# Who makes the lo parts of the q, k and v blocks, and how much dense product goes between the steps of the 16x16 inverses

## The chip, the cores and the metric

The kernel runs on one core of a Trainium2 chip. The metric is device time in microseconds (us) of one execution, lower is better. The engines are TensorE (PE: matrix products; PEld is its loading of weights), VectorE (DVE), ScalarE (ACT), GpSimd (POOL) and SyncE (SP, which here only issues transfers). Each engine has its own list of instructions.

## The reference

One layer of a mixed block on 512 tokens of width 1024: a token mixer, a cross-attention to a memory of 256 rows, and a mixture of 32 experts, each followed by a layer norm. The token mixer starts with one wide projection and has two branches. The branch that matters here is a gated delta rule in chunks. In short:

```python
proj = h @ w_in                                   # 512 x 8744
qkv  = silu(causal_dwconv(concat(g_q, g_k, g_v), conv_w))
q, k = l2_normalize(q) * dk**-0.5, l2_normalize(k)
a_mat = where(strict, (k @ k.T) * decay, 0) * beta
sol   = triangular_solve(a_mat + I, [v * beta, k * beta * exp(gc)])
# then a scan over chunks: v_new = u - w @ state;  o = q_dec @ state + qk @ v_new;  state = ...
```

For each of 8 heads and each chunk a unit lower triangular matrix has to be inverted, or solved with. The other branch is sparse attention (compressed, selected and windowed keys). Its projections come out of the same wide product.

## The kernel before, in words

**Dense products.** `w_in` is cut into blocks of 256 or 260 columns. Float32 precision is had with three passes: the weights and the activations are each written as a hi part and a lo part, and `mm3` (L209 to L213) multiplies hi by hi, hi by lo and lo by hi. One block is loaded by `load_w` (L140): a transfer of 1 MB into a raw buffer (L144, on SP's queue), then `split` for the parts: ScalarE writes the hi part (L138), and an engine named in the call subtracts it from the raw data to get the lo part (L139). The buffers come from a pool of 21 (`B8`, `NB8`), which hold also the matrices of the delta rule.

**The list of blocks.** `dense` (L187) is a generator that goes through the list `blocks`. It asks for the load of block j+1 when it starts block j, then yields after each step of block j. A step is one `mm3`: for a block worked by channel (the q, k, v blocks, C_K, C_V, S_K, W_K) it is 128 by 128 by 512 and counted as 0.65 us, with two column groups (c = 0 and 1) of 8 steps each; for a block worked by token (S_V, W_V) it is 256 columns wide and counted as 0.32 us, with 32 steps. The order of the first blocks is z3, k00, k01, S_V, W_V, q00, q01, v00, v01, k10, k11, q10, C_V, q11, v10, v11, C_K, S_K, W_K. In a name such as q01 the first digit is the half of the heads, the second the block in that half. After the 8 steps of one column group of a q, k or v block `conv_silu` (L417) follows: one ScalarE instruction (L421), three of VectorE (L424), one of ScalarE (L427), one of VectorE (L428), and then a set of four transposes on TensorE (L217). The product of a column group lies in one of two PSUM buffers ("mm").

**The weave.** `Weave.chain` runs another generator (the delta rule's inverse, its scan, later the sparse attention) and, at each of its yields, takes steps from `dense` until their counted time uses up the yielded number. `W.until(label)` works dense steps off until the named block is through. The part of the program that the change touches is

```python
W.until("k01");  W.chain(gdn_inverse(0), "k11")
W.until("v01");  W.chain(gdn_scan(0), "q11")
W.until("k11");  W.chain(gdn_inverse(1), "n6160")
W.until("v11");  W.chain(gdn_scan(1))
```

**The inverse.** `gdn_inverse` (L473) works on four heads at once. It first makes the decay and the matrices AN, with a yield of ZA after each of four heads. Then it inverts all the 16x16 diagonal blocks by forward substitution, 15 steps of one VectorE multiplication (L534) and one VectorE sum (L535), each waiting for the one before; after every third step it yields ZB, five times in all. Two passes then spread the result into the block layout (L542 to L547: XC and then XTC), with a yield of ZC after each. Then TensorE's part begins: 128 small products of 32x32 (L554), which need XC, and in further stages (L560, L564, L575, L584, L589, L596, L605) the 32x32 blocks become the full 128x128 inverse, with yields ZD, ZE and fixed ones. GpSimd masks the blocks for L554 (L520) and clears XT (L521).

```python
for c in range(1, 16):
    V.tensor_tensor(tv, yb[:, 0:c, 0:c], nb[:, c, 0:c, None]..., op=OP.mult)   # L534
    V.tensor_reduce(yb[:, c, 0:c], tv..., axis=AX.X, op=OP.add)                 # L535
    if c % 3 == 0:
        yield ZB
```

**What sets the order.** The program is written down in the order of the weave; a planner then fixes each engine's list at build time, by the order in the text and by when it expects each instruction's data to be ready. On the chip every engine works its list off.

**POOL_PARTS.** Ten blocks (q00, q01, v00, v01, k10, k11, q10, q11, v10, v11) have their lo part made by GpSimd, all others by VectorE; the choice is made in `dense` at the call of `load_w`.

Of the kernel before, what the change touches and what calls it, by code (L numbers as in the profile page):

```python
# [91 lines left out]
def _body(ctx, tc, nc, I, O, dbg):  # L92
# [28 lines left out]
    def B8(shape, dt=FT):  # L121
        return big.tile(shape, dt, name="b8", bufs=NB8)
# [18 lines left out]
    def load_w(src, c0, n, eng=V, loads=1, splits=1):  # L141
        raw = B8([128, KD, WB])
        for k in pieces(loads):
            nc.sync.dma_start(raw[:, k, :n], src[128 * k.start:128 * k.stop, c0:c0 + n].rearrange("(k p) c -> p k c", p=128))  # L144
        hi = B8([128, KD, WB], FR)
        lo = B8([128, KD, WB], FR)
        for k in pieces(splits):
            split(hi[:, k, :n], lo[:, k, :n], raw[:, k, :n], eng)
        return hi, lo
# [23 lines left out]
    def dense(blocks, cur=None):  # L173


        load = lambda b: load_w(*b[1:4], eng=G if b[0] in POOL_PARTS else V, splits=SPL.get(b[0], 1))
        cur = cur or load(blocks[0])
# [686 lines left out]
    def nsa():  # L864
        wait, n = [], 0
        for h in range(H):
            W.until(HEAD[h])
            if h == 6:
                MT.update((n_, [B8([128, 4, S], FR) for _ in range(2)]) for n_ in "hl")
                MT["w"] = load_w(I["w_out"][0], 0, 256, eng=G if "w" in POOL_PARTS else V)  # L870
            for t in range(NT):
# [760 lines left out]


SPL = {"k00": 2}
ZA, ZB, ZC, ZD, ZE = 2.0, 2.5, 1.5, 1.4, 2.0
NB8, KBACK, PSP = 21, 6, 12
KB_LAST, KD_LAST = 3, 7
L0, L1 = 6, 8
# [3 lines left out]

GATES = ("m0", "z0", "m4", "m1", "m5", "z1", "m2", "z2", "m6", "m3", "m7")
HEAD = ("m4", "m5", "z1", "m2", "m6", "m3", "m7", "m7")
POOL_PARTS = ("q00", "q01", "v00", "v01", "k10", "k11", "q10", "q11", "v10", "v11")

_INS = ["x", "mem", "positions", "w_in", "gdn_conv_w", "gdn_a_log", "gdn_dt_bias", "gdn_norm_w", "cmp_pe", "cmp_w1",
        "cmp_b1", "cmp_w2", "w_out", "ln1_g", "ln1_b", "xa_wq", "xa_wkv", "xa_wo", "ln2_g", "ln2_b", "moe_w_group",
# [14 lines left out]
```

## Time and profile before

| | us |
|---|---|
| median of 3 runs | 1255.44 (1253.97 to 1255.5) |
| the profiled execution, its own time | 1254.66 |
| its span, first to last instruction | 1252.9 |
| TensorE busy in it | 1161.7 |
| VectorE busy | 658.2 |
| ScalarE busy | 459.3 |
| GpSimd busy | 181.9 |

The profile shows one execution. Its busy times are sums over the whole span; a stretch of the span has limits of its own, which the views by stretch (busy time of each engine, and the TensorE clock that was granted, as a share of full speed) and the lists of waits show. A wait "A <- B" is time in which A's engine had nothing running and B's instruction ended it. The delta rule's first inverse lies at about 59 to 138 us of the span, its first scan at 164 to 209, the second inverse at 210 to 304, the second scan from there to about 350.

### The profile page before, as it was taken

The page shows a single profiled execution, that of the slowest core. Times are in us where ns is not written, and L with a number is a line of the kernel's source. Part 1 is how long each engine was busy: PE and PEld are TensorE (multiplying, and loading weights), DVE is VectorE, ACT ScalarE, POOL GpSimd, SP SyncE. Part 2 cuts the span into 40 slices and gives each one's busy share as a digit, 9 for nine tenths or more (in the row PEclk, how much of TensorE's full clock was granted, in tenths as well). Part 3 has the DMA queues.
Part 4 walks back from the last instruction along what each step waited for, and adds up shares of the span by engine and source line. Part 5 has one row for each costly group of instructions (what it writes and reads, how often), then busy time and mean ns, then how long its engine had stood idle before and what let it go on. Part 6 is the DMA issues. An engine that isn't in the chain of part 4 may idle for free. (4 is left out here: it accounts for less than half of the span.)

```text
span 1252.9 us, 20776 instructions
## 1 busy us (share of the span) xinstructions
PE 1161.7 (93%) x8356; PEld 925.4 (74%) x8356; DVE 658.2 (53%) x1657; ACT 459.3 (37%) x1093; POOL 181.9 (15%) x151
## 2 busy tenths in 40 slices
PE   6996998879999999999899899999989999999994
PEld 6885787758888879999798799789985455455532
DVE  4695477874775724556457758233484111111147
ACT  4643454534544214343345524334142111111224
POOL 4151221221000000000001102000020000000185
PEclk9998999989999999999899999999998999999997
DMA  8220212112142562212531343227546899999823
GB/s 268 68 68 3 68 34 69 34 35 69 39 131 69 173 212 69 69 35 67 187 93 58 122 120 101 68 67 255 204 145 248 302 384 380 407 392 379 338 77 133
DMA packets 101882, 189.22 MB, mean 151 GB/s; under 512 B 10246, under 2 KB 74438, under 8 KB 97680
## 3 DMA queue, kind: packets, MB, share of 16 engines
q1 hardware_dynamic: 93456, 181.58, 41.1%
q0 software_dynamic: 2224, 3.94, 1.0%
q10 hardware_dynamic: 6096, 2.27, 0.8%
q8 instruction: 68, 1.11, 0.4%
q14 instruction: 38, 0.31, 0.1%
HBM read 177.93 MB, written 13.63 MB: 153 GB/s over the span
## 5 line engine op out<-in xcount | busy, mean ns | idle before, releaser
L211 PE MATMUL mm<-b,b 128*128 128x256 f32 (+3 forms) x1216 | 404.2, 333 | 21.7 <-ACT b L138 7.2
L212 PE MATMUL mm<-b,b 128*128 128x256 f32 (+3 forms) x1216 | 392.2, 323 | 2.2 <-DVE b L139 2.2
L213 PE MATMUL mm<-b,b 128*128 128x256 f32 (+3 forms) x1216 | 391.5, 322 | 0.7 <-POOL b L139 0.4
L211 PEld LDWEIGHTS mm<-b,b 128*128 128x128 f32 x1216 | 233.1, 192 | 43.3 <-issue 17.1
L213 PEld LDWEIGHTS mm<-b,b 128*128 128x128 f32 x1216 | 233.1, 192 | 22.1 <-issue 3.8
L212 PEld LDWEIGHTS mm<-b,b 128*128 128x128 f32 x1216 | 233.7, 192 | 18.2 <-DVE b L139 2.8
L1447 PE MATMUL ga<-b,b 128*64 128x512 f32 x512 | 131.5, 608 | 6.8 <-DVE b L1334 6.8
L139 DVE TENSOR_TENSOR b<-b,b 128x2048 fp32r<-128x2048 f32 (+4 forms) x48 | 101.8, 2123 | 56.5 <-ACT b L138 48.0
L138 ACT ACTIVATE b<-b 128x2048 fp32r<-128x2048 f32 (+4 forms) x58 | 104.3, 1799 | 26.9 <-DMA b<-in_w_in_dram 7.4
L1447 PEld LDWEIGHTS ga<-b,b 128*64 128x64 f32 x512 | 38.4, 138 | 73.8 <-issue 64.1
L424 DVE SCALAR_TENSOR_TENSOR t<-mm,cw,t 128x511 f32<-128x511 f32 (+2 forms) x72 | 53.8, 747 | 32.3 <-ACT t L421 31.1
L217 PE MATMUL tp<-cs,b 128*128 128x128 f32 x376 | 59.4, 287 | 9.7 <-DMA cs<-in_cst_dram 5.9
L1462 PE MATMUL ga<-b,t 128*64 128x512 f32 x256 | 63.9, 593 | 0.5 <-ACT t L1306 0.5
L139 POOL TENSOR_TENSOR b<-b,b 128x2048 fp32r<-128x2048 f32 x10 | 45.9, 4593 | 123.2 <-ACT b L138 102.1
L1327 PE MATMUL mm<-t,b 128*128 128x256 f32 x240 | 61.5, 294 | 0.0
L1299 DVE SCALAR_TENSOR_TENSOR t<-t,ga 128x256 f32<-128x256 f32 x16 | 6.7, 420 | 98.2 <-ACT t L1298 98.1
L217 PEld LDWEIGHTS tp<-cs,b 128*128 128x128 f32 x376 | 45.4, 147 | 15.3 <-DMA cs<-in_cst_dram 5.9
L1327 PEld LDWEIGHTS mm<-t,b 128*128 128x128 f32 x240 | 48.8, 203 | 0.8 <-issue 0.8
L1462 PEld LDWEIGHTS ga<-b,t 128*64 128x64 f32 x256 | 20.0, 137 | 36.2 <-issue 35.1
L815 POOL MEMSET b<- 128x97 f32 x32 | 5.6, 179 | 272.6 <-PE ga L762 170.7
L1310 POOL DMA_INDIRECT ybuf<-b,idx x14 | 13.7, 980 | 215.4 <-ACT b L1470 111.2
L1306 ACT ACTIVATE t<-tp 128x256 f32<-128x256 f32 x16 | 6.1, 383 | 88.8 <-PE tp L217 88.8
(442 smaller groups left out, 1842.4 us busy)
## 6 DMA issues: line engine op xcount, KB each, us to landing
b<-in_moe_w_gate_dram SPq DMA_DIRECT2D x64, 512.0 KB, 10.3
b<-in_moe_w_up_dram SPq DMA_DIRECT2D x64, 512.0 KB, 10.7
b<-in_moe_w_down_dram SPq DMA_DIRECT2D x32, 1024.0 KB, 12.6
b<-in_w_in_dram SPq DMA_DIRECT2D x22, 1024.0 KB, 5.3
b<-in_w_in_dram SPq DMA_DIRECT2D x10, 1040.0 KB, 5.2
b<-in_cmp_w_dram SPq DMA_DIRECT2D x16, 512.0 KB, 8.4
b<-in_xa_wkv_dram SPq DMA_DIRECT2D x8, 1024.0 KB, 5.3
ybuf<-t SPq DMA_DIRECT2D x1, 4096.0 KB
```

What stands on the lines that cost most here:

```text
L138: A.activation(hi, src, AF.Copy)
L139: eng.tensor_tensor(lo, src, hi.bitcast(FT), op=OP.subtract)
L211: T.matmul(out, wh, xh, start=first, stop=False)
L212: T.matmul(out, wh, xl, start=False, stop=False)
L213: T.matmul(out, wl, xh, start=False, stop=last)
L217: T.transpose(dst_psum[:, i * 128:(i + 1) * 128], s_, ident)
L424: V.scalar_tensor_tensor(acc[:, s_:], pp[:, :S - s_], cw[:, c_:c_ + 1], acc[:, s_:], op0=OP.mult, op1=OP.add)
L1299: V.scalar_tensor_tensor(th, th, 1.0, ph[:, :256], op0=OP.add, op1=OP.mult)
L1310: G.indirect_dma_start(out=ybuf[:, :], out_offset=bass.IndirectOffsetOnAxis(ap=idx, axis=0), in_=yt, in_offset=None, bounds_check=2 * S - ...
L1327: T.matmul(p, rows_of(hl)(t)[:, c], sv, start=False, stop=t == NT - 1)
L1447: T.matmul(ph[64 * i:64 * i + 64], xg[:, k, 128 * pp + 64 * i:128 * pp + 64 * i + 64], WT[2 * pr + i, k // 4][:, :, k % 4], start=k == 0, ...
L1462: T.matmul(py[64 * i:64 * i + 64], hT[:, k, 64 * i:64 * i + 64], WT[2 * pr + i, 2][:, k, 512 * n:512 * n + 512], start=k == 0, stop=k == 1)
```

## The change

VectorE makes the lo parts of all ten blocks that GpSimd made before. The yield after every third substitution step of the inverse grows from 2.5 to 4.0, and the one after each of the two spreading passes from 1.5 to 2.5. Nothing else is altered.

```diff
-ZA, ZB, ZC, ZD, ZE = 2.0, 2.5, 1.5, 1.4, 2.0
+ZA, ZB, ZC, ZD, ZE = 2.0, 4.0, 2.5, 1.4, 2.0
...
-POOL_PARTS = ("q00", "q01", "v00", "v01", "k10", "k11", "q10", "q11", "v10", "v11")
+POOL_PARTS = ()
```

The line that reads the tuple, in `dense`, is

```python
load = lambda b: load_w(*b[1:4], eng=G if b[0] in POOL_PARTS else V, splits=SPL.get(b[0], 1))
```

## Rows read from the trace of the kernel before

**Rows 1.** The page's first part: busy us, share of the span, instructions.

```profile
PE 1161.7 (93%) x8356; PEld 925.4 (74%) x8356; DVE 658.2 (53%) x1657; ACT 459.3 (37%) x1093; POOL 181.9 (15%) x151
```

**Rows 2.** TensorE's waits, stretches 58:150, 138:224 and 220:340: total, times, longest.

```profile
PE ga L554 <- DVE b L547: 9.0, 1, 9.0
...
PE mm L211 <- DVE t L424: 3.6, 1, 3.6
...
PE ga L554 <- DVE b L547: 6.1, 1, 6.1
PE mm L211 <- DVE t L424: 2.9, 1, 2.9
...
PE mm L211 <- DVE t L535: 1.8, 1, 1.8
```

**Rows 3.** Busy us by stretch: PE, PEld, DVE, ACT, POOL; clock, DMA share, GB/s.

```profile
101.80:107.30 5.50, 5.43 (x137) 4.38 (x137) 3.40 (x7) 1.28 (x2) 0.00 (x0) 0.57 0.01 3
...
215.70:220.00 4.30, 4.30 (x15) 3.45 (x16) 2.85 (x4) 3.38 (x14) 0.00 (x0) 0.60 0.01 2
...
248.80:252.00 3.20, 3.20 (x16) 2.63 (x17) 2.96 (x10) 3.20 (x10) 0.81 (x1) 1.00 0.00 0
...
268.10:274.70 6.60, 6.54 (x142) 5.00 (x142) 5.02 (x8) 2.60 (x3) 0.00 (x0) 0.57 0.01 2
...
77.40:104.20 26.80, 17.79 (x240) 16.31 (x239) 25.39 (x45) 5.48 (x7) 14.95 (x7) 0.85 0.25 79
```

**Rows 4.** TensorE's timeline: start us, duration us, instruction; in brackets the wait before.

```profile
88.53 0.40 PE L211 MATMUL mm<-b,b 128*128 128x512 f32 x1
...
92.00 0.40 PE L211 MATMUL mm<-b,b 128*128 128x512 f32 x1
...
101.87 1.93 PE L554 MATMUL ga<-b 32*32 32x32 f32 x128 [9.01 <-DVE b L547]
...
151.91 0.65 PE L217 MATMUL tp<-cs,t 128*128 128x128 f32 x4
```

**Rows 5.** VectorE's timeline around the lo parts on GpSimd.

```profile
83.61 4.59 DVE L534 TENSOR_TENSOR t<-t,t 128x49 f32<-128x49 f32 x1
...
89.09 0.24 DVE L534 TENSOR_TENSOR t<-t,t 128x81 f32<-128x81 f32 x1
...
206.28 0.16 DVE L225 SCALAR_TENSOR_TENSOR rs__2106<-q,rs__2106 128x4 f32<-128x4 f32 x1
...
207.46 4.47 DVE L225 SCALAR_TENSOR_TENSOR rs__2106<-q,rs__2106 128x4 f32<-128x4 f32 x1
...
251.30 4.61 DVE L534 TENSOR_TENSOR t<-t,t 128x81 f32<-128x81 f32 x1
```

**Rows 6.** GpSimd's timeline.

```profile
83.54 4.60 POOL L139 TENSOR_TENSOR b<-b,b 128x2048 fp32r<-128x2048 f32 x1
...
207.33 4.58 POOL L139 TENSOR_TENSOR b<-b,b 128x2048 fp32r<-128x2048 f32 x1 [35.95 <-ACT b L138]
...
251.19 4.61 POOL L139 TENSOR_TENSOR b<-b,b 128x2048 fp32r<-128x2048 f32 x1 [3.76 <-ACT b L138]
```

**Rows 7.** Groups by line and shape, whole span: busy us, mean ns; idle before.

```profile
L139 DVE TENSOR_TENSOR b<-b,b 128x2048 fp32r<-128x2048 f32 x31 | 70.9, 2288 | 38.7 <-ACT b L138 38.4 <-PE ga L807 0.4
...
L139 POOL TENSOR_TENSOR b<-b,b 128x2048 fp32r<-128x2048 f32 x10 | 45.9, 4593 | 123.2 <-ACT b L138 102.1 <-PE mm L212 21.0
...
L424 DVE SCALAR_TENSOR_TENSOR t<-mm,cw,t 128x510 f32<-128x510 f32 x24 | 18.0, 748 | 0.6
...
L428 DVE SCALAR_TENSOR_TENSOR b<-t,t 128x512 f32<-128x512 f32 x16 | 12.6, 790 | 11.0 <-ACT t L427 11.0
```

**Rows 8.** A lo part on VectorE; ScalarE's hi part; the transfer of a block.

```profile
316.93 2.29 DVE L139 TENSOR_TENSOR b<-b,b 128x2048 fp32r<-128x2048 f32 x1 [2.75 <-ACT b L138]
...
79.78 1.91 ACT L138 ACTIVATE b<-b 128x2048 fp32r<-128x2048 f32 x1
...
b<-in_w_in_dram SPq DMA_DIRECT2D x22, 1024.0 KB, 5.3
```

## The prediction

> **What bounds the kernel now.** The page's first part comes first: TensorE is busy for 1161.7 of 1252.9 us [rows 1], so time can be won only where TensorE stands idle, some 91 us in all, or runs slowly. The list of TensorE's waits then says where the change can reach. In each of the two inverses TensorE stands once before the first small products (L554), which need XC from VectorE: 9.0 us in the first inverse and 6.1 in the second [rows 2]. In the first scan a dense product waits 3.6 us for L424, in the second inverse there are two more such waits of 2.9 and 1.8 [rows 2]. The stretches show what follows: behind these waits TensorE works at a granted clock of 0.57 (101.8 to 107.3), 0.57 (268.1 to 274.7) and 0.60 (215.7 to 220.0) of full speed, a mixture of its two levels (1.2 and 2.4 GHz); behind the wait of 1.8 us the clock stays at 1.00 [rows 3].
>
> Why is XC late? VectorE's timeline tells it. A substitution product of 81 elements takes 0.24 us in the first inverse and 4.61 us in the second; one of 49 elements takes 4.59 us in the first [rows 5]. In both cases the long one starts just after a lo part begins on GpSimd (83.54 and 251.19) and ends when that lo part ends [rows 6]. So a small VectorE operation with both inputs in SBUF waits for the whole GpSimd instruction, 4.61 - 0.24 = 4.4 us longer. There are two such stretched steps in each inverse, 8.7 us of each chain, and a third case in the scan: 4.47 us for an instruction that takes 0.16 beside it [rows 5, 6].
>
> The Trainium skill (SBUF — State Buffer, section "SBUF: two separate sides") says that GpSimd and a VectorE operation with two SBUF inputs share a port pair as an exclusive lock, held for the whole instruction; the rows agree, with 4.61 us against 0.24.
>
> **The change, part by part.** All ten lo parts move. On GpSimd each takes 4.6 us, on VectorE 2.29 [rows 7]: VectorE gets 22.9 us of work over about 240 us and loses the stretched steps. The raw buffer is given back 2.3 us earlier, so SP's transfers start no later; GpSimd keeps L520 and the clearing of XT, and nothing is left on it that these could delay.
>
> *How many products move.* I counted the yields as the weave takes them. Ahead of L554 in the first inverse the text of before has 64 steps of S_V and W_V and 8 of q00; the last one taken is written behind the yield, so 7 products of 512 columns should stand there, and the timeline has just 7, the second at 88.53 and the last at 92.00, so 0.694 us a step [rows 4]. TensorE's list follows the text here. With the new numbers it is 24 steps of q00 and q01: 16 more, 16 x 0.694 = 11.1 us, and two sets of transposes of 0.65 [rows 4], 12.4 us. In the second inverse it is 59 steps in place of 42: 17 x 0.694 = 11.8, and two sets, 13.1 us. These products come out of the runs that stood before the scans (36 steps become 20, 18 become 1); where those end, the state is the same as before, so everything from the second scan on keeps its order, and the sum of TensorE's work doesn't change.
>
> *What reaches the chain.* The column groups that now finish inside the chain bring their conv_silu: 3 x 0.748 + 0.790 = 3.03 us of VectorE each [rows 7], two in each inverse. Lo parts that fall ahead of XC: q00, q01, v00 in the first, q11, v10, v11 in the second, 3 x 2.29 = 6.9 us each.
>
> - First inverse: idle time left = 9.0 (before) - 8.7 (stretched steps gone) + 6.9 (lo parts) + 6.1 (conv) - 12.4 (products in the gap) = 0.9. Won: 8.1.
> - Second: 6.1 - 8.7 + 6.9 + 6.1 - 13.1 = -2.7, so nothing is left. Won: 6.1.
> - The clock behind the two gaps. In 5.5 us at 0.57 the lower level holds for 2 x 0.43 x 5.5 = 4.7 us, half of which is lost: 2.4; in 6.6 us it is 2.8 [rows 3]. An idle time of 0.9 is less than the 1.8 after which the clock stayed at 1.00. Won: 5.2.
> - The first scan: the stretch of 4.3 (4.47 - 0.16) becomes a lo part of 2.3, so the wait of 3.6 falls to 1.6 [rows 2, 5]. Won: 2.0, and the lower clock after it, 2 x 0.40 x 4.3 / 2 = 1.7 [rows 3]. Together 3.7; between 0 (the lo part stands in the same place) and 5.3 (all of it goes).
> - What is late next: a dense product whose PSUM buffer VectorE still reads. The waits of 2.9 and 1.8 of the second inverse are of this kind, behind both of q10's column groups. The change puts four more column groups among the chains. No row shows them there: from below none waits, from above all four, 4 x 2.35 and two falls of the clock, 12.8. I take the half, since one of the two rows lost clock and one didn't: 2 x 2.35 + 1.7 = 6.4 lost.
>
> Sum: 8.1 + 6.1 + 5.2 + 3.7 - 6.4 = 16.7 us won. On the profiled execution's own time that is 1254.66 - 16.7 = 1238.0; the median of the runs is 0.8 higher, so **1238.8 us**.
>
> The parts don't add up. Only the lo parts: 9.0 - 8.7 + 4.6 = 4.9 and 6.1 - 8.7 + 4.6 = 2.0 us of idle time left. Only the products, lo parts on GpSimd: 9.0 + 6.1 - 12.4 = 2.7 and 6.1 + 6.1 - 13.1 = 0. Either alone closes more than half of the two gaps, so the forecast doesn't hang on one of them.
>
> **A rule against it.** In the chain VectorE is busy for 25.39 of 26.8 us [rows 3], and GpSimd is mostly free. The Trainium skill (Perfetto Trace Analysis, section "Optimizing Scalar/DVE Operations") says that where VectorE is saturated, handing work to ScalarE or even GpSimd may make sense, and warns that between VectorE and GpSimd it might not help. Read without the warning, the change takes work back to the engine that is full. The row of 4.61 us speaks for the warning: 8.7 us of the 25.39 are waiting on GpSimd and no work. By the unwarned rule the sum would be that of the third rival, 1262.
>
> **The rivals.**
>
> 1. *VectorE becomes the bound.* It holds conv_silu, lo parts and the chain at once; for it speaks that it is full now in the chain, against it that 8.7 us of that go. Price: a third conv_silu of 3.0 stands ahead of XC in each inverse (idle left 3.9 and 0.3), the first gap still costs its clock, and all four PSUM waits come: won 5.1 + 5.8 + 2.8 + 3.7 - 12.8 = 4.6, so 1250.8; 1246 to 1254 with its parts.
> 2. *Slower: lo parts hold up VectorE's list.* A lo part needs ScalarE's hi part, that needs the landed block (1.9 and 5.3 us [rows 8]). If the planner sets the lo part early in VectorE's list, chain and conv_silu stand behind it for w us. Its place is the three lo parts of each inverse: idle time 0.9 + 3w and -2.7 + 3w, the clock is not won back; with the scan's 3.7 and the 6.4 the sum is 6w - 14.2, so it decides from w = 2.4. One lo part waited 2.75 us in VectorE's list (at 316.93 [rows 8]). At w = 7.2, hi part and transfer in full, it is +29.0: 1284. Against it: over the 31 lo parts that VectorE makes now the wait is 38.7 / 31 = 1.2 [rows 7], and on GpSimd the hi parts came in time for TensorE.
> 3. *The stretching doesn't go away*: GpSimd's work costs VectorE nothing, and what VectorE takes back adds to its chain in full. Then 9.0 + 6.9 + 6.1 - 12.4 = 9.6 and 6.1 + 6.9 + 6.1 - 13.1 = 6.0 are left, 0.5 more than before, with the 6.4: 1262. Rows 5 and 6 are all against it. It is also what the sentence of the Trainium skill on handing work over (Perfetto Trace Analysis, the same section) would give without its warning.
> 4. *The planner doesn't follow the text*, and TensorE's list keeps its 7 products ahead of L554. Then only the lo parts act: 4.1 + 4.1, the second gap's clock 2.8, the scan 3.7: 14.7 won, 1240.7. The count of 7 speaks against it.
>
> **How the numbers follow.** Forecast 0.67, rivals 0.17, 0.10, 0.03, 0.03. A measurement of this kernel can tell about 0.2% from no change, 2.5 us. Faster by more than that: forecast, rival 4 and two thirds of rival 1, 0.81; within it 0.06, the rest of rival 1; slower 0.13, rivals 2 and 3. Range: with no new PSUM waits 1238.8 - 6.4 = 1232.4, and with a part of the old ones gone (2.9 + 1.8 and the clock behind them are 6.4 again, to 1226) 1228 at the lower end; at the upper end the middle of rival 1, 1251.
>
> **What would show it.** Right: no L139 on POOL; no L534 over 1 us; L554's wait at most 2 us in each inverse; 23 products of 512 columns ahead of the first L554; the clock at 1.00 behind L554; total TensorE idle 12 to 20 us less. Wrong: lo parts on VectorE with long waits for L138 inside the chains (rival 2); new waits of L211 for L424 of over 6 us together (rival 1); stretched steps that stay, behind something else than lo parts (rival 3).

## The result, and the profile after

The changed kernel takes 1240.38 us, the median of 4 runs (1234.19 to 1246.97). The kernel before took 1255.47 beside it (1253.97 to 1259.03). The ratio is 0.9865, with a 95% interval of 0.984 to 0.9891 (the two medians alone give 0.988). The profiled execution is the fastest of the four, 1234.19 us with a span of 1232.1; the median lies 6.2 us above it, which matters below.

The page's first part (busy us, share of the span, instructions) answers to [rows 1]: GpSimd lost 46.5 us, VectorE has no more than before, and TensorE's work is the same.

```profile
PE 1161.6 (94%) x8356; PEld 925.9 (75%) x8356; DVE 655.9 (53%) x1667; ACT 458.9 (37%) x1093; POOL 135.4 (11%) x141
```

VectorE has ten instructions more, 22.9 us of lo parts, and its sum is 2.3 us below the old one. So some 25 us of stretching went. TensorE's sum is the same in a span that is 20.8 us shorter (1252.9 to 1232.1), so in this execution the whole gain is idle time.

TensorE's waits from 58 to 346 us, which covers both inverses and both scans (total, times, longest). They answer to [rows 2], whose waits come to 15.1 us for L554 and 6.6 for L424 over this stretch:

```profile
PE mm L211 <- DVE t L424: 3.5, 2, 3.1
PE ga L564 <- issue: 2.8, 2, 2.3
PE mm L213 <- DVE b L139: 1.7, 1, 1.7
...
PE tp L217 <- DVE t L428: 1.0, 1, 1.0
PE mm L211 <- DVE t L535: 0.6, 1, 0.6
PE ga L560 <- issue: 0.5, 1, 0.5
```

L554's two waits are gone altogether. The scan's 3.6 us for L424 shrank to 0.4, and the 3.1 that is left stands in the second inverse, where a wait of 2.9 stood [rows 2]. One wait is new: 1.7 us for a lo part (L139); for the lo parts on GpSimd TensorE had waited 0.4.

VectorE's timeline of the first inverse (start, duration, instruction) answers to [rows 5]:

```profile
83.66 0.21 DVE L534 TENSOR_TENSOR t<-t,t 128x49 f32<-128x49 f32 x1
...
84.75 0.24 DVE L534 TENSOR_TENSOR t<-t,t 128x81 f32<-128x81 f32 x1
...
87.83 2.28 DVE L139 TENSOR_TENSOR b<-b,b 128x2048 fp32r<-128x2048 f32 x1
...
92.35 2.28 DVE L139 TENSOR_TENSOR b<-b,b 128x2048 fp32r<-128x2048 f32 x1
...
101.19 0.69 DVE L547 TENSOR_TENSOR b<-t,cs 128x512 f32<-128x512 f32 x1
```

The step of 49 elements that took 4.59 takes 0.21. Two lo parts of 2.28 and the first `conv_silu` stand in the chain instead, and VectorE waits for ScalarE ahead of that `conv_silu`. So XC, which this L547 writes, is ready at 101.88. Before it was ready at 101.82:

```profile
101.13 0.69 DVE L547 TENSOR_TENSOR b<-t,cs 128x512 f32<-128x512 f32 x1
```

TensorE's timeline of the same stretch answers to [rows 4]:

```profile
87.83 0.40 PE L211 MATMUL mm<-b,b 128*128 128x512 f32 x1
...
105.58 0.39 PE L211 MATMUL mm<-b,b 128*128 128x512 f32 x1
...
106.36 1.29 PE L554 MATMUL ga<-b 32*32 32x32 f32 x128
...
116.34 0.26 PE L564 MATMUL ga<-b 32*32 32x32 f32 x8 [2.33 <-issue]
```

Between the first two rows, both included, lie 23 products of 512 columns in place of 7 (counted by their L211), and L554 follows without a wait, 4.5 us after XC. In the first inverse, then, XC comes no earlier than before, and TensorE spends the time until then on products. Ten microseconds on, L564 stops for 2.33 us ("issue": the profile shows nothing that it waited for).

What VectorE's lo parts waited for from 58 to 346 us (the list of VectorE's waits), over 16 of them:

```profile
DVE b L139 <- ACT b L138: 5.0, 4, 2.4
...
DVE b L139 <- PE mm L212: 1.3, 1, 1.3
```

The stretches (busy us of PE, PEld, DVE, ACT, POOL; then granted clock, DMA share, GB/s) bring the other half of the story. First before, then after:

```profile
58.00:346.00 288.00, 256.73 (x2512) 217.64 (x2512) 202.66 (x452) 128.65 (x360) 61.19 (x20) 0.96 0.16 50
...
118.00:128.00 10.00, 10.00 (x149) 8.09 (x146) 3.91 (x5) 5.68 (x8) 4.59 (x1) 1.00 0.01 2
```

```profile
58.00:346.00 288.00, 276.79 (x2615) 235.87 (x2613) 216.22 (x514) 139.27 (x392) 15.22 (x10) 0.96 0.19 59
...
118.00:128.00 10.00, 10.00 (x78) 7.58 (x77) 1.38 (x2) 4.85 (x15) 0.00 (x0) 0.52 0.01 1
```

TensorE's idle time in these 288 us falls from 31.3 to 11.2 us, by 20.1: nearly all of the 20.8 us by which the span became shorter. The granted clock over the stretch is 0.96 both times. The falls behind L554's waits are gone, but a new one stands at 118 to 128, behind L564's wait: 0.52 where it was 1.00 before. Before, L564 waited as long and kept the clock:

```profile
111.29 0.52 PE L564 MATMUL ga<-b 32*32 32x32 f32 x37 [2.22 <-issue]
```

### The profile page after: what moved, and what is told of

Read it like the earlier page. It is cut to its first block, busy times and chain, and to the rows that moved or that the text cites. A ratio compares the mean times of both kernels' runs of the same rounds, so it can differ in the third digit from the quotient of the medians.

```text
span 1232.1 us, 20783 instructions
## 1 busy us (share of the span) xinstructions
PE 1161.6 (94%) x8356; PEld 925.9 (75%) x8356; DVE 655.9 (53%) x1667; ACT 458.9 (37%) x1093; POOL 135.4 (11%) x141
## 5 line engine op out<-in xcount | busy, mean ns | idle before, releaser
L211 PE MATMUL mm<-b,b 128*128 128x256 f32 (+3 forms) x1216 | 404.1, 333 | 17.5 <-ACT b L138 7.4
L211 PEld LDWEIGHTS mm<-b,b 128*128 128x128 f32 x1216 | 233.3, 192 | 39.5 <-issue 13.2
L139 DVE TENSOR_TENSOR b<-b,b 128x2048 fp32r<-128x2048 f32 (+4 forms) x58 | 124.6, 2149 | 60.0 <-ACT b L138 50.1
L217 PE MATMUL tp<-cs,b 128*128 128x128 f32 x376 | 59.6, 288 | 9.3 <-DMA cs<-in_cst_dram 5.7
L424 DVE SCALAR_TENSOR_TENSOR t<-mm,cw,t 128x511 f32<-128x511 f32 (+2 forms) x72 | 53.7, 745 | 19.6 <-ACT t L421 18.4
L217 PEld LDWEIGHTS tp<-cs,b 128*128 128x128 f32 x376 | 45.9, 148 | 14.2 <-DMA cs<-in_cst_dram 5.6
L1326 PE MATMUL mm<-t,hh 128*128 128x256 f32 x120 | 35.7, 316 | 0.0
## 6 DMA issues: line engine op xcount, KB each, us to landing
b<-in_moe_w_down_dram SPq DMA_DIRECT2D x32, 1024.0 KB, 12.7
```

The costliest lines, as they stand in the source:

```text
L139: eng.tensor_tensor(lo, src, hi.bitcast(FT), op=OP.subtract)
L211: T.matmul(out, wh, xh, start=first, stop=False)
L217: T.transpose(dst_psum[:, i * 128:(i + 1) * 128], s_, ident)
L424: V.scalar_tensor_tensor(acc[:, s_:], pp[:, :S - s_], cw[:, c_:c_ + 1], acc[:, s_:], op0=OP.mult, op1=OP.add)
L1326: T.matmul(p, rows_of(hh)(t)[:, c], sv, start=t == 0, stop=False)
```

## The experiments

The theory: a lo part on GpSimd holds up VectorE's small SBUF operations for its whole length, and taking it away is the gain. Rivals: the gain is the products that now stand ahead of L554, or the two parts only work together. All kernels were timed beside the kernel before on the same chip; each number is a median with its runs, then the ratio to the kernel before and its 95% interval.

**The spread of the changed kernel.** The same kernel again, unchanged.

> The changed kernel once more, beside the others on one chip. Its four runs lay between 1234.2 and 1247.0 us, the kernel before between 1254.0 and 1259.0. Theory A (the spread is TensorE's clock, which falls in some executions behind the small products of the inverses and not in others): times between 1234 and 1247 again, and the mean clock of a run goes with its time: 0.01 less is about 10 us more. Rival (the spread is idle time, a wait that comes and goes): the times differ at the same mean clock.

Measured: 1245.68 us (1241.66 to 1252.87, 6 runs), 0.9916 (0.9885 to 0.9947). The three runs at a mean granted clock of 0.966 or 0.967 took 1241.66 to 1242.23, those at 0.957 to 0.961 took 1249.13 to 1252.87. Three runs lie above the 1247 of the forecast. The spread goes with TensorE's clock; more on it below.

**The lo parts alone.**

```diff
+POOL_PARTS = ()          # yields ZB, ZC stay 2.5, 1.5
```

> Only the lo parts move to VectorE; the yields stay at 2.5 and 1.5. Theory A (the two long waits ahead of L554 are VectorE's substitution steps stretched by lo parts on GpSimd): no L534 over 1.2 us, idle time ahead of L554 of 4.9 us in the first inverse and 2.0 in the second in place of 9.0 and 6.1, the scan's wait of 3.6 us gone or halved; 1241 us (1236 to 1247). Rival (the products in the gap are what counts): 1250 to 1256, the waits within 2 us of those before.

Measured: 1242.67 us (1236.85 to 1250.12, 6 runs), 0.9879 (0.9848 to 0.991), a time within Theory A's range. TensorE's waits from 58 to 346:

```profile
PE mm L211 <- DVE t L424: 3.6, 2, 3.1
...
PE mm L213 <- DVE b L139: 1.8, 1, 1.8
...
PE tp L217 <- DVE b L428: 1.5, 1, 1.5
...
PE ga L554 <- DVE b L547: 1.2, 1, 1.2
```

L554's waits fall from 15.1 to 1.2, without the larger yields. Of my 4.9 us left in the first inverse nothing came: XC was ready at 96.22, since the second lo part stands behind its L547 (at 96.39) and not ahead of it. TensorE was late itself: it waited for the first lo part, worked at the lower clock behind that (products of 0.63 us in place of 0.40), and reached L554 at 97.12, where it had been free from 92.9 on before. Of the 2.0 in the second inverse 1.2 came. VectorE's and TensorE's rows:

```profile
95.53 0.69 DVE L547 TENSOR_TENSOR b<-t,cs 128x512 f32<-128x512 f32 x1
```

```profile
90.96 0.50 PE L213 MATMUL mm<-b,b 128*128 128x512 f32 x1 [1.79 <-DVE b L139]
...
97.12 1.29 PE L554 MATMUL ga<-b 32*32 32x32 f32 x128
```

So the lo parts alone make XC 5.6 us earlier than before, where the changed kernel leaves it in its place.

**The products alone.**

```diff
-ZA, ZB, ZC, ZD, ZE = 2.0, 2.5, 1.5, 1.4, 2.0
+ZA, ZB, ZC, ZD, ZE = 2.0, 4.0, 2.5, 1.4, 2.0    # POOL_PARTS stays
```

> Only the yields grow to 4.0 and 2.5; GpSimd keeps the ten lo parts. Theory A (the parts are not additive, since the products cover the gap whatever opens it): two stretched L534 of over 4 us stay in each inverse, yet the wait ahead of L554 falls to 2.7 us or less in the first inverse and to 0 in the second; the scan's wait of about 3.6 us stays; 1244 to 1248 us. Rival (without the lo parts moved the chain is still late and conv_silu makes it later): waits ahead of L554 of 6 us and more, 1252 to 1258.

Measured: 1261.05 us (1259.56 to 1263.47, 12 runs), 1.0027 (1.0015 to 1.0038): a little slower than before, and slower than either theory forecast. TensorE's waits:

```profile
PE tp L217 <- DVE b L428: 11.1, 4, 4.3
PE mm L211 <- DVE t L424: 9.0, 3, 4.3
```

L554 waits no more, as forecast, and yet little is won. The late thing is now the transposes behind the products that were brought in, and the PSUM buffers. VectorE's timeline of this kernel says why:

```profile
90.08 4.55 DVE L534 TENSOR_TENSOR t<-t,t 128x121 f32<-128x121 f32 x1
...
98.56 2.31 DVE L424 SCALAR_TENSOR_TENSOR t<-mm,cw,t 128x511 f32<-128x511 f32 x3
...
102.23 0.65 DVE L428 SCALAR_TENSOR_TENSOR b<-t,t 128x512 f32<-128x512 f32 x1
```

and TensorE's:

```profile
102.94 1.12 PE L217 MATMUL tp<-cs,b 128*128 128x128 f32 x4 [4.32 <-DVE b L428]
```

`conv_silu` of the first column group stands in VectorE's list behind the substitution that GpSimd stretches, so products whose result VectorE must take are no cover for a late VectorE.

**Which lo parts count.** Six of them (q00, q01, v00, q11, v10, v11) fall beside the inverses' chains, four (v01, k10, k11, q10) outside. First the changed kernel with the four left on GpSimd, larger yields:

```diff
+POOL_PARTS = ("v01", "k10", "k11", "q10")
```

> The changed kernel, but GpSimd keeps the lo parts of v01, k10, k11 and q10, which fall outside the two chains of substitution steps; VectorE makes q00, q01, v00, q11, v10 and v11. Theory A (the stretched steps of the chains are what counted, the scan's share is small): no L534 over 1.2 us, no wait ahead of L554, but a VectorE instruction of over 4 us in the first scan and a TensorE wait of 2 to 4 us behind it; 1 to 5 us more than the changed kernel beside it. Rival (every lo part taken from GpSimd is worth the same): about four tenths of the gain lost, 1248 to 1254 us.

Measured: 1254.85 us (1250.93 to 1259.9, 10 runs), 0.9978 (0.9957 to 0.9999). Theory A failed: most of the gain is gone, where the rival had four tenths of it. VectorE's timeline:

```profile
114.84 3.82 DVE L428 SCALAR_TENSOR_TENSOR b<-t,t 128x512 f32<-128x512 f32 x1 [0.16 <-ACT t L427]
...
154.58 3.92 DVE L428 SCALAR_TENSOR_TENSOR t<-t,t 128x512 f32<-128x512 f32 x1 [0.76 <-ACT t L427]
...
161.49 0.69 DVE L428 SCALAR_TENSOR_TENSOR t<-t,t 128x512 f32<-128x512 f32 x1 [0.76 <-ACT t L427]
...
206.19 4.44 DVE L225 SCALAR_TENSOR_TENSOR rs__2106<-q,rs__2106 128x4 f32<-128x4 f32 x1
```

and TensorE's, where it stops for the first and the last of these:

```profile
118.72 1.11 PE L217 MATMUL tp<-cs,b 128*128 128x128 f32 x4 [2.65 <-DVE b L428]
...
214.39 0.77 PE L211 MATMUL mm<-b,b 128*128 128x512 f32 x1 [4.33 <-DVE t L424]
```

GpSimd's lo parts start at 113.61, 153.35, 163.34 and 206.06 here. Three of them meet such an instruction. Where one meets `conv_silu`'s L428 or the scan's norm (L225), that instruction takes 3.8 to 4.4 us in place of 0.69 or 0.16. So the place that counts is every one where VectorE owes TensorE something, not the inverse alone.

The same split with the yields of before, to size each half by itself:

```diff
+POOL_PARTS = ("q00", "q01", "v00", "q11", "v10", "v11")   # first kernel: the four outside on VectorE
+POOL_PARTS = ("v01", "k10", "k11", "q10")                 # second: the six inside on VectorE
```

> The kernel before, its yields too, but VectorE makes the lo parts of v01, k10, k11 and q10, which stand outside the inverses' chains; the six inside (q00, q01, v00, q11, v10, v11) stay on GpSimd. Theory A (the four outside are the larger half, as the run that left just these four on GpSimd lost some 10 us): 1245 to 1249 us, although the waits of L554 of 9.0 and 6.1 us stay; the instructions stretched in the scan (L225, L428) are back below 1 us. Rival B (the four outside matter only where more products stand in the chains; with the yields of before they cost what the scan's wait costs): 1251 to 1255 us, with the wait of L211 for L424 of 3.6 us gone or below 2.

> The kernel before, its yields too, but VectorE makes the lo parts of the six blocks inside the inverses' chains (q00, q01, v00, q11, v10, v11); v01, k10, k11 and q10 stay on GpSimd. Theory A (the four outside are the larger half): 1250 to 1255 us, though L554 waits under 3 us in both inverses together. Rival B (the chains are the larger half, as the prediction had it, and the loss of some 10 us came of the larger yields beside the four on GpSimd): 1243 to 1248 us.

Measured: the four outside on VectorE 1252.1 us (1250.22 to 1256.07, 10 runs), 0.9959 (0.9943 to 0.9976); the six inside 1255.18 (1245.01 to 1256.2, 10 runs), 0.9951 (0.992 to 0.9982). The first time lies where rival B had it, the second just above theory A's range. Neither half is clearly the larger, so neither theory stands. In gains the two are 0.0041 and 0.0049, together 0.0090, against 0.0121 for all ten; the intervals are too wide to tell whether they add up. TensorE's waits of the first:

```profile
PE ga L554 <- DVE b L547: 15.1, 2, 9.0
...
PE mm L211 <- DVE t L424: 3.6, 2, 3.1
```

and of the second:

```profile
PE tp L217 <- DVE b L428: 8.2, 3, 3.9
PE mm L211 <- DVE t L424: 2.3, 1, 2.3
...
PE ga L554 <- DVE b L547: 1.2, 1, 1.2
```

Each removes just the waits of its own places. In the second, 6.7 us more of L217's waits for L428 appear than in the lo parts alone, since GpSimd still meets L428.

**The length of GpSimd's instruction, not its work.** In the kernel before, GpSimd keeps its lo parts but makes each in 8 instructions of 256 columns.

```diff
+        if eng is G:
+            A.activation(hi[:, :, :n], raw[:, :, :n], AF.Copy)
+            for k in pieces(8):
+                G.tensor_tensor(lo[:, k, :n], raw[:, k, :n], hi[:, k, :n].bitcast(FT), op=OP.subtract)
+            return hi, lo
```

> The kernel before; GpSimd keeps its ten lo parts but makes each in 8 instructions of 256 columns in place of one of 2048. Theory A (a VectorE operation with two inputs in SBUF waits for the end of one GpSimd instruction, so what it loses goes with that instruction's length): the pieces take about 0.6 us, L534 is stretched by no more than that, so the longest is under 1.3 us; the chains win most of the 8.7 us, the waits ahead of L554 fall from 15.1 us to under 8; 1243 to 1252 us. Rival (GpSimd at work slows VectorE whatever the length): the steps during a lo part lose as much in sum, the waits ahead of L554 stay above 12 us, 1254 to 1260.

Measured: 1247.38 us (1246.07 to 1251.37, 4 runs), 0.991 (0.9879 to 0.994). Theory A held, though a piece takes 0.80 us and not 0.6. Lines lie 5 lower here (L534 is L539) and the lo part on GpSimd is L150. GpSimd's groups, then TensorE's waits, then the line of the substitution (min, median, max ns):

```profile
L150 POOL TENSOR_TENSOR b<-b,b 128x256 fp32r<-128x256 f32 x80 | 60.8, 796 | 104.7 <-ACT b L148 89.6 <-ACT t L581 14.8 <-POOL b L150 0.2
```

```profile
PE ga L559 <- DVE b L552: 5.4, 2, 4.3
```

```profile
L539 DVE TENSOR_TENSOR t<-t,t x30: 161/332/1135, 79.3 to 251.9; 128x1 f32<-128x1 f32 x2, 128x4 f32<-128x4 f32 x2, 128x9 f32<-128x9 f32 x2, 128x16 f32<-128x16 f32 x2
```

GpSimd is busier (60.8 us against 45.9 [rows 7]) and the kernel is faster. No substitution step takes more than 1.14 us; the wait ahead of the small products fell from 15.1 to 5.4. VectorE got no lo part to make in this kernel, so what it was spared is the waiting.

**Three attempts at the waits that remain.** A larger yield between the stages of small products; and C_V's products ahead of q10's, with the larger yields and without.

```diff
+ZA, ZB, ZC, ZD, ZE = 2.0, 4.0, 2.5, 3.9, 2.0
```

> The changed kernel with ZD 3.9 in place of 1.4: 6 dense steps in place of 3 behind L554 and behind L560. Theory A (in the changed kernel's profile the clock is 0.52 from 117.4 to 128.0, behind a stretch with mostly small products and a wait of 2.3 us, which costs 5.1 us; more dense work between them keeps it up): no stretch under 0.8 behind L564, 1229 to 1236 us and a smaller spread of the runs. Rival (the fall comes from the wait of 2.3 us in L564 alone, or by chance): the stretch at about half the clock stays, 1238 to 1243.

```diff
-... + P3("k", 1) + [gdn_proj(1,"q",0)] + NP(C_V) + ...
+... + P3("k", 1) + NP(C_V) + [gdn_proj(1,"q",0)] + ...
```

> The changed kernel with the block C_V, which needs no conv_silu, ahead of q10 in the list, so that the products among the second inverse's first instructions bring VectorE nothing. Theory A (products help only as far as what follows them doesn't stand behind VectorE's list): the wait of L211 for L424 of 3.1 us at the second inverse's start falls under 1 us and the clock behind it stays up; 1 to 6 us less than the changed kernel in the mean. Rival (q10's conv_silu then meets the substitution steps and another wait takes its place): no less TensorE idle time, no difference.

> The kernel with the lo parts alone moved (yields 2.5 and 1.5), and C_V ahead of q10 as in the run before this one. Theory A: as there, the wait of 3.1 us at the second inverse's start goes; 1235 to 1242 us, not distinguishable from the run before this one. Rival (the yields matter once C_V is used up earlier): it is slower than that run by 3 us and more, with waits ahead of the second L554 of 3 us and more.

Measured: 1248.63 us (0.9924, 0.9898 to 0.995), 1245.57 (0.9898, 0.9862 to 0.9933) and 1244.65 (0.9888, 0.986 to 0.9917). The first is slower than both its theories had it: it shortened the fall at 118 to 128 (0.85 there), but its wait of L211 for L424 is 5.5 us. The second went as its rival said, the third lies above its forecast. Each of the two with C_V first brought that group down to 0.4, and waits for a lo part came in its place; of the second:

```profile
PE mm L213 <- DVE b L139: 4.8, 2, 3.0
...
PE mm L211 <- DVE t L424: 0.4, 1, 0.4
```

No version here beats the changed kernel beyond its interval.

**What the larger yields are worth.** The changed kernel and the lo parts alone, side by side once more.

> The changed kernel once more, in more rounds, beside the kernel with the lo parts alone. Theory A (the larger yields leave some 3 us less idle time but the clock takes as much back): its median within 3 us of the other's, both 1240 to 1247 us, and their ratios to the kernel before overlap. Rival B (the larger yields are worth their idle time): it is faster by 3 us or more.

> The lo parts alone, with the yields of before, once more, in more rounds. Theory A (the larger yields are worth nothing that can be measured): 1240 to 1247 us, within 3 us of the changed kernel. Rival B (they are worth their idle time): slower than the changed kernel by 3 us or more.

Measured: 1243.1 us (1240.44 to 1252.49, 6 runs), 0.9884 (0.9851 to 0.9917), against 1243.67 (1238.28 to 1248.12, 6 runs), 0.9878 (0.9851 to 0.9905). Theory A held: nothing that can be measured. Over all runs the medians are 1242.15 (16 runs) and 1243.26 (12 runs).

**Idle time and clock, kernel by kernel.** From 58 to 346 us, each from one profiled execution (the ratio is that of all its runs): TensorE's idle time, and the time at the lower level of the clock (1.2 GHz), summed over stretches of 6 us as 2 x (1 - granted clock) x 6. Half of the latter is lost.

| kernel | idle us | lower level us | ratio |
|---|---|---|---|
| before | 31.3 | 23.8 | 1 |
| after | 11.2 | 20.4 | 0.9865 |
| after, second time | 12.0 | 27.2 | 0.9916 |
| after, third time | 12.4 | 47.9 | 0.9884 |
| lo parts alone | 14.7 | 30.7 | 0.9879 |
| lo parts alone, second time | 16.7 | 30.7 | 0.9878 |
| products alone | 28.8 | 40.8 | 1.0027 |
| changed kernel, four outside on GpSimd | 21.5 | 30.7 | 0.9978 |
| before, GpSimd in pieces | 22.3 | 27.4 | 0.991 |
| four outside on VectorE | 26.2 | 20.5 | 0.9959 |
| six inside on VectorE | 18.7 | 27.2 | 0.9951 |

The products alone win 2.5 us of idle time and lose 8.5 to the clock ((40.8 - 23.8) / 2), hence slower. The three executions of the changed kernel agree in their idle time within 1.2 us, and differ by 27.5 us at the lower level.

## Why the prediction was right, and where not

It said 1238.8 us, within 1228 to 1251; 1240.38 was measured, and 1243 to 1246 in the later runs. By its own steps:

- **The stretched steps** go, as said: no L534 above 1.14 us, where each inverse had two of 4.2 to 4.6. (The 1.14 is a step of 4 elements beside GpSimd's L520, which is there before and after.) Against the clean steps of the changed kernel the stretching was 8.6 and 8.2 us, not 8.7 twice. That this is the cause, and not the engine's load, is shown by the eight pieces: the same work on GpSimd, and 0.991.
- **Gaps ahead of L554**: 0.9 and 0 were predicted, 0 and 0 measured; 15.1 won, 14.2 predicted. The 23 products are there. In the first inverse only two of the three lo parts and one of the two `conv_silu` stood ahead of XC, so that TensorE came 4.5 us after XC and not 0.9 before it; in the second all of them did, and it came 0.3 after it (262.61 and 262.91), not 2.7.
- **The first scan**: the wait went from 3.6 to 0.4, not to 1.6, so 3.2 and not 2.0.
- **New PSUM waits**, 4.7 us and 1.7 for a clock fall: mis-sized. The only groups of this kind that remain are the old ones (2.9 and 1.8 [rows 2] became 3.1 and 0.6). The four column groups brought into the chains added no wait, since `conv_silu` was in time once VectorE wasn't stretched.
- **The clock**: this term of the sum failed. I took 5.2 us behind L554 and 1.7 behind the scan's wait as won, and nothing new but 1.7. The falls there did go, but 10 us at 0.52 came at 118. From 58 to 346 us the clock gave (23.8 - 20.4) / 2 = 1.7 us in the first profiled execution, in the third one it took (47.9 - 23.8) / 2 = 12.1. Over the whole span TensorE was busy for 1161.6, 1166.4 and 1173.3 us in the three executions of the changed kernel, against 1161.7 before: nothing won, up to 11.6 lost.
- **The sum**: idle time was predicted to fall by 8.1 + 6.1 + 2.0 - 4.7 = 11.5 us and fell by 20.1 (over the whole span by 20.7, where 12 to 20 were named as the sign of being right); the clock was to give 5.2 and gave 1.7 or took. With opposite signs the errors nearly cancel in the median: 16.7 predicted, 15.1 measured. The mechanism was right, two sizes were off, and that they cancel so well is luck.
- **"Either alone closes more than half of the two gaps"**: this step failed for the products. They close both gaps and make the kernel slower, 1.0027, because they bring VectorE work that is late by the same stretch. I had counted idle time at L554 only, and not what the products' own results wait for. For the lo parts it holds: they alone bring the whole gain.
- **The scan's share**, 3.7 us, for all that lies outside the chains: with the yields of before the four lo parts there are worth 0.0041, about 5 us (3 to 7), so 3.7 is within reach. Beside the larger yields it is too small: leaving them on GpSimd costs the changed kernel most of its gain. I had seen L225 stretched and not looked for L428.
- **The rivals.** VectorE did not become the bound: no PSUM wait was added. Lo parts held up VectorE's list by 6.3 us over 16 of them, 0.4 each, far from 2.4. The stretching went. The planner did follow the text, though rival 4's time for the lo parts alone, 1240.7, is near what these gave (1242.67 and 1243.67).

The rule that I weighed (the Trainium skill, Perfetto Trace Analysis, section "Optimizing Scalar/DVE Operations") warns that handing VectorE's work to GpSimd might not help. The runs agree with the warning: ten lo parts on GpSimd cost 1.2% of this kernel.

What stays open is why L564's "issue" wait of about 2.2 us, which is there before and after, costs the clock in one and not in the other. The wait itself has a companion in the record of transfers: within 0.5 us ahead of its start a transfer of about 16 KB on the queue called "instruction" ran (at 108.6 before, at 113.7 in the changed kernel, at 113.5 in its third execution). Others, as the one at 117.4 in the changed kernel, have no stop behind them. Whether TensorE waits there for its own instructions no run tested.

## What to carry to other kernels

Ahead of giving GpSimd a long elementwise instruction, list what VectorE does beside it and who waits for that; a short instruction of VectorE on a chain can wait for the whole of it, and cutting the long one into pieces is a cheap test. Dense products between the steps of a chain are cover only if their own results don't need the engine that is late. And where a change removes idle time, look at the clock in several executions before its return is counted in the sum.

## What the hardware showed unexpectedly

**The clock differs between executions of one program.** The stretch from 58 to 346 us of the changed kernel's third profiled execution, and two stretches inside:

```profile
58.00:346.00 288.00, 275.64 (x2557) 233.94 (x2556) 207.13 (x491) 133.66 (x381) 15.26 (x10) 0.92 0.19 57
...
118.00:128.00 10.00, 10.00 (x80) 7.85 (x79) 1.15 (x2) 4.46 (x14) 0.00 (x0) 0.50 0.00 0
128.00:138.00 10.00, 10.00 (x108) 8.10 (x107) 2.93 (x4) 2.58 (x5) 0.00 (x0) 0.50 0.36 107
```

and of the first:

```profile
128.00:138.00 10.00, 10.00 (x147) 8.16 (x145) 3.62 (x5) 3.07 (x5) 0.00 (x0) 1.00 0.34 105
```

TensorE waits in the same places for nearly as long (L424 3.5 us in both, L564 2.7 and 2.8, L535 1.7 and 0.6). Yet the fall behind L564 lasts through 118 to 138 in the one, and ends near 128 in the other. The clock of the stretch is 0.92 against 0.96, which is 288 x 0.04 = 11.5 us of the 12.7 by which the spans differ (1244.8 and 1232.1). Over the 16 runs of this kernel a mean clock lower by 0.01 goes with 10.5 us more (correlation -0.95). The kernel with the six inside on VectorE fell into two groups: four runs of 1245.01 to 1246.67 at 0.967 to 0.97, six of 1255.03 to 1256.2 at 0.961 or 0.962. The Trainium skill (TensorE: Matmul & The Clock Gate, section "Part 1: The HAM clock gate") says that the slow phase at a kernel's start differs from run to run of one kernel and counts it as under 1% of a typical span. The traces agree on the variation; the 11.5 us here are 0.9% of the span, and lie in the middle of a program.

**What GpSimd stretches.** Not only two-tensor operations of VectorE: with the products alone, L542, one tensor times a value per partition, took 4.60 us for two in place of 0.79 (108.08), beside a lo part that began at 107.69. And not every GpSimd instruction stretches: beside L521, which only clears a buffer, the substitution steps kept 0.17 to 0.20 us, and L424, which reads PSUM and one tensor, kept 1.53 for two beside a lo part at 122.46 in the kernel before. The Trainium skill (SBUF — State Buffer, section "SBUF: two separate sides") names VectorE's operations in a two-port mode beside those with two SBUF inputs, and for the latter counts only a GpSimd operation that reads SBUF. The row of L521 fits that. The row of L542 fits if L542 works in such a mode, which no run here shows.
